# Token tiles moved by one DMA over 128 partitions instead of four over 32, and the lambda vectors loaded later

## The chip, the cores and the metric

One NeuronCore of a Trainium2 chip runs the whole program. The metric is device time in microseconds (us) of one execution; the time given for a kernel is the median of its runs. A profiled execution is one more run, recorded instruction by instruction, and has its own time.

## What is computed

Two layers of a hybrid backbone act on 1024 latent tokens `x` and 256 context tokens `ctx`, each token a row of 1024 float32 numbers. Layer 0 mixes tokens by differential attention, layer 1 by a bidirectional state-space layer (S5); each mixer is followed by a squared-ReLU MLP of width 4096, and both are wrapped in RMS norms with shift, scale and gate from a small projection of `c` ("ada").

```python
h = rmsnorm(x, norm_g[i, 0]) * (1.0 + s1) + sh1
y_lat, y_ctx = diff_attention(h_lat, h_ctx, ...) if i == 0 else s5_mixer(...)
x = x + g1 * rmsnorm(y_lat, norm_g[i, 1])
h = rmsnorm(x, norm_g[i, 2]) * (1.0 + s2) + sh2
x = x + g2 * rmsnorm(sqrelu_mlp(h, mlp_w1[i], mlp_w2[i]), norm_g[i, 3])
# in diff_attention:
lam = exp(sum(lf[0] * lf[1])) - exp(sum(lf[2] * lf[3])) + lambda_init
w = p[:, :, 0] - lam * p[:, :, 1]
```

The change touches how rows of `x`, `ctx` and two intermediate copies (`xa`, `xb`) travel between DRAM and SBUF, and when `lam` is computed.

## The kernel before

**Tokens and tiles.** The 1280 tokens form ten tiles of 128 (tiles 0 to 7 latent, 8 and 9 context). A token's number is taken apart as `8c + 2sh + sl`, with `sh` from 0 to 3 and `sl` 0 or 1. A tile holds one `sl` and 32 values of `c`; on the SBUF side its partition is `32 sh + c`. So in SBUF a tile is 128 partitions by 1024 numbers (4 KB a row, 512 KB in all), and in DRAM it is four blocks (`sh`), two tokens apart, of 32 rows, eight tokens apart. `tile_dma` (line 278) moves it as four DMAs of 32 partitions, 128 KB each. `pair_dma` (line 291) loads the two tiles with `sl` = 0 and 1 at once, as four DMAs of 256 KB: rows of 8 KB, 1 MB in all.

**Queue.** Every DMA is issued by `dma` (line 79) from one engine, SP, in one order. SP waits in that order for what each DMA needs, so a DMA that waits holds back all behind it. The order on SP and on the other engines is laid out when the program is built, by a planner with costs of its own, except inside `manual()` blocks, where the order of the source holds.

**Stages that the change and the prediction touch:**

- `setup` (line 155) and `lam_setup` (line 486) come first. `lam_setup` loads the four lambda vectors, broadcast to all partitions (128 KB into the buffer FC), and the sub-norm gains (0.5 KB), and computes `neglam`, `sg` and `ones` with nine small VectorE and two ScalarE instructions. Their first use is in the attention stage (lines 554, 672, 705).
- `phase_v` (line 339): V projection. `v_norm` (line 326) loads pairs 0 and 1 of `x` at the start, pairs 2 and 3 after the first group's products, pair 4 (context) after the second group's features; each tile is squared and summed on ScalarE (line 149), scaled on GpSimd (line 335), transposed on TensorE (line 314), modulated (lines 317, 319) and split into a high and a low part (lines 137, 138). The modulation needs `ada_w` (lines 237 to 263), and the products (lines 132 to 134) need split weights from `attn_w_qkv`. All these loads stand in SP's queue behind the first two pairs.
- `phase_b`: attention, in a hand-written order.
- `phase_c` (line 1246): output projection by `attn_w_o`, residual and MLP norm. `finish` (line 1260) loads tile `i` of `x` into one of three buffers, adds to it (line 1277), stores the sum to `xa` (line 1278), and takes its norm (line 1284). The load of the tile three places on goes into the same buffer, so it waits for that store. `feature` (line 1288) then transposes the finished tiles of a group; the last group's tiles go to `second_group` (line 1331).
- `mlp0_down` with `m0_tile` (line 1688): the first MLP's end. `first` loads a tile of `xa` (line 1700), `residual` adds it and stores tiles 0 to 7 to `xb` (line 1720). `mlp0_end` (line 1739) does the last five tiles in a hand-written order, with `xa` loads from line 1746, and hands over to the S5 stage, whose `rotate` (line 1853) writes over buffers that the last `xb` stores read.

Of the kernel before, what the change touches and what calls it, by code (L numbers as in the profile page):

```python
# [61 lines left out]
class Ring:  # L62
# [3 lines left out]
    def next(self):  # L66
        self.i += 1
        return self.items[self.i % len(self.items)]


class Prog:
# [206 lines left out]
    def tile_dma(self, dram, i, slot, store=False):  # L278

        d = dram[1] if i >= 8 else dram[0]  # L280
        src = d.rearrange("(c sh sl) d -> sl sh c d", sh=4, sl=2)[i % 2]
        if i < 8:
            src = src[:, 32 * (i // 2) : 32 * (i // 2) + 32]
        for sh in range(4):
            s = slot[32 * sh : 32 * sh + 32]
            if store:
                self.dma(src[sh], s)
            else:
                self.dma(s, src[sh])

    def pair_dma(self, dram, pair, slot):

        src = (dram[1] if pair == 4 else dram[0]).rearrange("(c sh sl) d -> sh c (sl d)", sh=4, sl=2)
        if pair < 4:
            src = src[:, 32 * pair : 32 * pair + 32]
        for sh in range(4):
            self.dma(slot[32 * sh : 32 * sh + 32].rearrange("p a b -> p (a b)"), src[sh])

    G_TOK = (512, 512, 256)
    G_TILES = ((0, 1, 2, 3), (4, 5, 6, 7), (8, 9))  # L300
# [38 lines left out]
    def phase_v(self):  # L339
        nc, I = self.nc, self.I  # L340
        self.xs = Ring([self.f0(8.5 + 8 * i, 2, 1024) for i in range(4)] + [self.fv(0, 2, 1024)])
        tmps = [Ring([v(o, 512), v(o + 2, 512)]) for v, o in ((self.fv, 0), (self.wv, 12), (self.wv, 12))]
        self.hT = self.hgroups()
        A, B = self.modc[:, 0, 1], self.modc[:, 0, 0]
        banks = [Ring([self.bank(i) for i in b]) for b in ((4, 6), (4, 6, 7), (4, 6, 7))]
        proj = Ring([self.bank(i) for i in range(4)])
        wr = [(self.rv(51 - 8 * i, 2, 512), self.rv(55 - 8 * i, 2, 512)) for i in range(4)]
        wt = [(hi[:, j], lo[:, j]) for hi, lo in wr for j in range(2)]
        wq = I["attn_w_qkv"][0].rearrange("(k p) n -> p k n", p=128)
        stg = Ring([self.rv(x, 2, 512) for x in (19, 23)])  # L350

        def load(ring, nb, order=range(4)):
            raws = [ring.next() for _ in order]
            for kk, raw in zip(order, raws):
                self.dma(shaped(raw, (2, 512)), wq[:, 2 * kk : 2 * kk + 2, 2048 + 512 * nb : 2560 + 512 * nb])
            return raws

        def weights(raws, order, engs):
            for raw, kk, eng in zip(raws, order, engs):
                hi, lo = wr[kk]  # L360
                self.split(hi, lo, shaped(raw, (2, 512)), eng)

        def feature(g, k, eng=None):
            m = 1 if g == 2 else 0
            self.to_feature(tiles[g], A[:, m], B[:, m], self.hT[g][0], self.hT[g][1], banks[g], tmps[g], k, eng, k % 2 == 1)

        def product(b, g, i, k, ks=range(8)):
            hh, hl = (t[:, k, 128 * i : 128 * i + 128] for t in self.hT[g])
            self.mm3(b, hh, hl, wt[k][0], wt[k][1], k == ks[0], k == ks[-1])

        def out(b, nb, g, i):
            kt = (2 + 4 * g + i) if g < 2 else i
            s = stg.next()
            nc.scalar.activation(s[:, 0], b, AF.Copy)
            nc.vector.tensor_tensor(s[:, 1], b, s[:, 0].bitcast(F32), ALU.subtract)
            for h in range(2):
                self.dma(self.Vd[4 * nb : 4 * nb + 4, h, :, kt].rearrange("h p e -> p h e"),
                         s[:, h].bitcast(F32).rearrange("p (h e) -> p h e", h=4))

        tiles = [self.v_norm(0)]  # L380
        acc = self.bank(5)
        for half in range(2):
            for seg in (1, 0):
                self.ada_half(0, seg, half, self.bank(5 if seg else 7))
            kk = range(2 * half, 2 * half + 2)
            weights(load(self.raw, 0, kk), kk, [nc.vector if half else nc.gpsimd] * 2)
        self.raw = Ring([self.wv(4 * i, 1024) for i in range(3)] + [self.view(self.SP, 4 * i, (1024,)) for i in range(3)])
        self.bg = [self.interleave([self.ada(0, seg, acc) for seg in (2, 3, 4)] + [self.rows_out(0, acc)],
                                   [self.s5_prep()])]
        bs = [proj.next() for _ in range(4)]  # L390
        for k in range(8):
            feature(0, k, nc.vector)
            for i in range(4):
                product(bs[i], 0, i, k)
        tiles.append(self.v_norm(1))
        for i in range(4):
            out(bs[i], 0, 0, i)
        for k in range(8):
            feature(1, k)
            self.step()  # L400
        tiles.append(self.v_norm(2))
        raws = load(Ring([self.f0(32.5, 1024), self.f0(36.5, 1024)]), 1, (3, 2))
        tok = [(g, i) for g in range(3) for i in range(len(self.G_TILES[g]))]
        for nb in range(2):
            for n, (g, i) in enumerate(tok[4 * (1 - nb) :]):
                if nb == 0 and n < 2:
                    for k in range(4 * n, 4 * n + 4):
                        feature(2, k)
                b = proj.next()
                ks = range(7, -1, -1) if (nb, n) in ((0, 5), (1, 0)) else range(8)  # L410
                for k in ks:
                    product(b, g, i, k, ks)
                if nb == 0 and n == 1:
                    raws += load(Ring([self.fv(0, 1024), self.fv(4, 1024)]), 1, (1, 0))
                elif nb == 0 and n == 5:
                    weights(raws, range(3, -1, -1), [None] * 4)
                out(b, nb, g, i)
                if nb and n == 1:
                    queries = self.b_start()
                if nb and n:  # L420
                    next(queries, None)
                self.step(6 if nb and n else 7)
        self.drain()
        for _ in queries:
            pass
# [59 lines left out]

    def lam_setup(self):
        nc, I = self.nc, self.I
        t, pr = self.fv(0, 256), self.fv(1, 2, 64)
        self.dma(t, I["attn_lambda"].rearrange("o a b -> o (a b)").to_broadcast((128, 256)))
        t4 = shaped(t, (2, 2, 64))  # L490
        nc.vector.tensor_tensor(pr, t4[:, :, 0], t4[:, :, 1], ALU.mult)
        st = self.lamc = self.cst.tile([128, 12], F32, name="lamc")
        nc.vector.tensor_reduce(st[:, 0:2], pr, AX.X, ALU.add)
        nc.scalar.activation(st[:, 2:4], st[:, 0:2], AF.Exp)
        nc.scalar.activation(st[:, 4:6], st[:, 2:4], AF.Ln)
        nc.vector.tensor_tensor(st[:, 4:6], st[:, 0:2], st[:, 4:6], ALU.subtract)
        nc.vector.tensor_scalar(st[:, 4:6], st[:, 4:6], 1.0, None, ALU.add)
        nc.vector.tensor_tensor(st[:, 2:4], st[:, 2:4], st[:, 4:6], ALU.mult)
        nc.vector.tensor_tensor(st[:, 6:7], st[:, 3:4], st[:, 2:3], ALU.subtract)
        nc.vector.tensor_scalar(st[:, 6:7], st[:, 6:7], -0.2, None, ALU.add)  # L500
        self.neglam = st[:, 6:7]
        self.dma(st[:, 7:8], I["attn_subln"].rearrange("o e -> e o"))
        nc.vector.tensor_scalar(st[:, 7:8], st[:, 7:8], 0.8, None, ALU.mult)
        self.sg = st[:, 7:8]
        self.ones = st[:, 8:9]
        nc.vector.memset(self.ones, 1.0)
# [937 lines left out]
    def a_out(self, run, p, t):  # L1444
        self.dma(self.A0[run][p], t)
# [908 lines left out]
    def run(self):  # L2354
        tc = self.tc
        pool = lambda name, **kw: tc.tile_pool(name=name, bufs=1, **kw)
        with pool("cst") as self.cst, pool("psp", space=bass.MemoryType.PSUM) as psp, \
# [22 lines left out]
            with pool("r0") as rp, pool("fc") as cp:  # L2380
                self.R, self.F = rp.tile([128, 59 * KB], F32R, name="R0"), cp.tile([128, 8 * KB], F32, name="FC")
                with pool("f0") as fp, pool("sp") as sp:
                    self.F0, self.SP = fp.tile([128, 41 * KB], F32, name="F0"), sp.tile([128, 12 * KB], F32, name="SP")
                    self.f0 = lambda off, *dims: self.view(self.F0, off, dims)
                    self.setup()
                    self.lam_setup()
                    more = [self.view(self.SP, 4 * i, (1024,)) for i in range(3)]
                    self.raw = Ring([self.wv(4 * i, 1024) for i in range(4)] + [self.f0(24.5 + 4 * i, 1024) for i in range(4)] + more)
                    self.phase_v()
# [78 lines left out]
```

## Time and profile before

| | |
|---|---|
| median of three runs | 2880.2 us (2878.24 to 2882.3) |
| the profiled execution's own time | 2870.1 us |
| its span, first to last instruction | 2868.3 us |
| mean granted TensorE clock | 0.989 |
| DMA queue of SP | 447564 packets, 583.53 MB, 63.9% of 16 engines' time |
| `x` in pairs | 16 DMAs of 256 KB from `x` and 4 from `ctx` |
| `x` and `ctx` in tiles | 40 DMAs of 128 KB |
| `xa` stores, `xa` loads, `xb` stores | 40, 40 and 32 DMAs of 128 KB |

Rows of the profile start with the time in us from the span's start and the duration, then engine, source line, operation, output and inputs; brackets give the idle time of the engine ahead of the instruction and what ended it. SP's DMA rows (SPq) are the issue alone. In a table by window, the columns are the busy us of each engine with its count, the granted clock (PEclk, 1.00 is full speed), the mean busy share of the 16 DMA engines, and GB/s.

### The profile page before, as it was taken

The numbers are of one execution on the slowest core, as the hardware profiler recorded it, in microseconds if no ns is written. First come the engines' busy times: TensorE is split into PE (matmuls) and PEld (weight loads), VectorE is DVE, ScalarE is ACT, GpSimd is POOL, SyncE is SP. The second block draws the span as 40 slices with busy tenths as digits, with TensorE's granted clock in tenths as the row PEclk, the third lists the DMA queues.
The fourth block names the chain that finished last, engine by engine and source line by source line (L and its number), as shares of the span: only waits on it lengthen the run. The fifth ranks groups of instructions, "written<-read, shape, count | busy, mean of one in ns | idle before, by whom it ended". The sixth has DMA issues, their size and how long they took to land. (4 is left out here: it accounts for less than half of the span.)

```text
span 2868.3 us, 43597 instructions
## 1 busy us (share of the span) xinstructions
PE 2730.3 (95%) x15225; PEld 2281.8 (80%) x15225; DVE 2016.2 (70%) x2968; ACT 1363.1 (48%) x2551; POOL 1021.6 (36%) x899
## 2 busy tenths in 40 slices
PE   7999999999899999999999999789999999999999
PEld 4688888888777887878877778688788778878887
DVE  5456788888863666666788767799533597668456
ACT  3425556555554743333444335477444633344443
POOL 2314666676663600000010013588121243336314
PEclk9999999999999999999999999899999999999999
DMA  9955555555826468885899887479743144466544
GB/s 299 309 169 175 153 173 175 177 175 169 255 83 190 120 212 306 296 305 192 272 294 299 260 244 242 156 232 295 253 140 110 59 159 164 158 235 235 165 131 141
DMA packets 447786, 586.33 MB, mean 204 GB/s; under 512 B 60494, under 2 KB 293196, under 8 KB 444364
## 3 DMA queue, kind: packets, MB, share of 16 engines
q1 hardware_dynamic: 447564, 583.53, 63.9%
q8 instruction: 120, 1.97, 0.3%
q14 instruction: 102, 0.84, 0.1%
HBM read 396.38 MB, written 182.82 MB: 202 GB/s over the span
## 5 line engine op out<-in xcount | busy, mean ns | idle before, releaser
L132 PE MATMUL PS<-H 128*128 128x512 f32 x1056 | 416.0, 395 | 8.6 <-DVE FD L1620 5.7
L134 PE MATMUL PS<-H 128*128 128x512 f32 x1056 | 413.8, 393 | 1.6 <-DVE H L2139 1.3
L133 PE MATMUL PS<-H 128*128 128x512 f32 x1056 | 414.8, 393 | 0.0
L132 PE MATMUL PS<-H,R 128*128 128x512 f32 (+1 forms) x828 | 307.5, 374 | 3.6 <-ACT R L137 1.6
L133 PE MATMUL PS<-H,R 128*128 128x512 f32 (+1 forms) x828 | 298.2, 360 | 1.4 <-POOL H L138 1.4
L134 PE MATMUL PS<-H,R 128*128 128x512 f32 (+1 forms) x828 | 297.6, 360 | 0.0
L132 PEld LDWEIGHTS PS<-H 128*128 128x128 f32 x1056 | 199.4, 189 | 55.0 <-issue 6.4
L134 PEld LDWEIGHTS PS<-H 128*128 128x128 f32 x1056 | 199.6, 189 | 45.3 <-DVE H L2139 1.7
L133 PEld LDWEIGHTS PS<-H 128*128 128x128 f32 x1056 | 199.7, 189 | 41.5 <-issue 1.0
L545 ACT ACTIVATE F<-F,stat 128x1280 f32<-128x1280 f32 x128 | 174.4, 1363 | 106.2 <-DVE F L535 105.9
L132 PE MATMUL PS<-R,H 128*128 128x512 f32 x536 | 213.6, 401 | 1.4 <-ACT R L137 1.4
L137 ACT ACTIVATE R<-W 128x512 fp32r<-128x512 f32 (+1 forms) x186 | 130.8, 712 | 172.3 <-PE PS L133 99.2
L133 PE MATMUL PS<-R,H 128*128 128x512 f32 x536 | 210.9, 394 | 0.0
L134 PE MATMUL PS<-R,H 128*128 128x512 f32 x536 | 209.3, 394 | 1.7 <-DVE H L138 1.7
L137 ACT ACTIVATE H<-U 128x640 fp32r<-128x640 f32 x216 | 132.9, 678 | 150.9 <-PE PS L133 104.5
L138 DVE TENSOR_TENSOR H<-W,H 128x512 fp32r<-128x512 f32 (+1 forms) x137 | 124.2, 917 | 103.8 <-ACT H L137 103.1
L138 DVE TENSOR_TENSOR H<-U,H 128x640 fp32r<-128x640 f32 x216 | 165.9, 805 | 39.7 <-ACT H L137 37.8
L535 DVE TENSOR_SCALAR_CACHE_REDUCE F<-PS 128x1280 f32<-128x1280 f32 x128 | 185.2, 1483 | 8.6 <-PE PS L522 8.4
L137 ACT ACTIVATE H<-W 128x512 fp32r<-128x512 f32 (+2 forms) x158 | 96.1, 616 | 191.2 <-PE PS L133 114.3
L132 PEld LDWEIGHTS PS<-H,R 128*128 128x128 f32 x828 | 156.8, 190 | 29.7 <-issue 4.1
L134 PEld LDWEIGHTS PS<-H,R 128*128 128x128 f32 x828 | 156.8, 189 | 25.4 <-issue 0.8
L582 POOL TENSOR_SCALAR R<-F 128x256 fp32r<-128x256 f32 (+1 forms) x128 | 127.1, 993 | 134.3 <-ACT F L581 121.5
(514 smaller groups left out, 6830.0 us busy)
## 6 DMA issues: line engine op xcount, KB each, us to landing
W<-in_mlp_w SPq DMA_DIRECT2D x176, 256.0 KB, 3.0
U<-Aa SPq DMA_DIRECT2D x108, 320.0 KB, 4.5
Aa<-FU SPq DMA_DIRECT2D x91, 320.0 KB, 4.6
Ad<-F SPq DMA_DIRECT2D x112, 256.0 KB, 3.0
W<-Ad SPq DMA_DIRECT2D x112, 256.0 KB, 2.8
FU<-in_mlp_w SPq DMA_DIRECT2D x32, 512.0 KB, 5.5
Ta<-FU SPq DMA_DIRECT2D x16, 1024.0 KB, 3.9
recd<-U SPq DMA_DIRECT2D x64, 256.0 KB, 4.8
```

Source lines behind the costliest of these rows:

```text
L132: mm(out, ah, bh, start=first, stop=False, **kw)
L133: mm(out, ah, bl, start=False, stop=False, **kw)
L134: mm(out, al, bh, start=False, stop=last, **kw)
L137: self.nc.scalar.activation(hi, src, AF.Copy)
L138: (lo_eng or self.nc.vector).tensor_tensor(lo, src, hi.bitcast(F32), ALU.subtract)
L535: ts(p[c], self.PS[:, 1280 * c : 1280 * c + 1280], 1.0, None, ALU.mult, ALU.min, accum_out=sm[:, c : c + 1])
L545: nc.scalar.activation(p[c], p[c], AF.Exp, bias=sm[:, c : c + 1], scale=-1.0, accum_out=sn[:, 0:1] if c else s0[:, u + 1 : u + 2])
L582: nc.gpsimd.tensor_scalar(hi, t, 1.0, 0.0, ALU.mult, ALU.add)
```

## The change

Both helpers hand the whole tile or pair to one DMA: the DRAM side is a pattern of 4 by 32 rows, the SBUF side all 128 partitions. This replaces 172 DMAs by 43. `lam_setup` moves from before `phase_v` to its loop over the second weight block: it stands after the split of those weights, and its scratch space is moved to a place in FC that this split has just read.

```diff
@@ tile_dma
-        for sh in range(4):
-            s = slot[32 * sh : 32 * sh + 32]
-            if store:
-                self.dma(src[sh], s)
-            else:
-                self.dma(s, src[sh])
+        if store:
+            self.dma(src, slot)
+        else:
+            self.dma(slot, src)
@@ pair_dma
-        for sh in range(4):
-            self.dma(slot[32 * sh : 32 * sh + 32].rearrange("p a b -> p (a b)"), src[sh])
+        self.dma(slot.rearrange("p a b -> p (a b)"), src)
@@ phase_v
                 elif nb == 0 and n == 5:
                     weights(raws, range(3, -1, -1), [None] * 4)
+                    self.lam_setup()
@@ lam_setup
-        t, pr = self.fv(0, 256), self.fv(1, 2, 64)
+        t, pr = self.fv(6, 256), self.fv(7, 2, 64)
@@ run
                     self.setup()
-                    self.lam_setup()
```

## Prediction, made before the changed kernel was run

> **What bounds the kernel now.** I read the page first (busy times, the 40 slices, the chain that ended last), then windows where these tiles move, then SP's order and who waits for what.
>
> ```profile
> span 2868.3 us, 43597 instructions
> PE 2730.3 (95%) x15225; PEld 2281.8 (80%) x15225; DVE 2016.2 (70%) x2968; ACT 1363.1 (48%) x2551; POOL 1021.6 (36%) x899
> PE   7999999999899999999999999789999999999999
> DMA  9955555555826468885899887479743144466544
> PE 29%; DVE 4%; DMA 2%; ACT 1%; issue 1%; POOL 0%; SPq 0%; DVEq 0%; POOLq 0%; ACTq 0%
> ```
>
> TensorE is busy 95% of the span, so a transfer costs time only where PE or the chain waits for it: slice 1 (PE 7, DMA 9) and slice 26 (PE 7, around 1830 us). SP's own issuing has no share of the chain (SPq 0%), so 129 issues fewer buy nothing by themselves.
>
> The price of a transfer comes from windows (columns: length, busy us of PE, PEld, DVE, ACT, POOL, clock, DMA share, GB/s).
>
> ```profile
> 4.00:16.00 12.00, 0.70 (x4) 0.47 (x3) 2.18 (x11) 3.67 (x7) 2.08 (x5) 1.00 0.96 196
> 20.00:45.00 25.00, 20.27 (x269) 13.44 (x272) 13.46 (x49) 7.57 (x10) 8.46 (x6) 1.00 1.05 405
> 50.00:62.00 12.00, 12.00 (x79) 8.98 (x78) 11.03 (x39) 6.27 (x11) 3.21 (x6) 1.00 1.00 231
> 908.25:911.80 3.55, 3.55 (x18) 2.93 (x17) 0.69 (x1) 3.50 (x7) 1.65 (x4) 1.00 0.55 148
> 908.00:966.00 58.00, 56.28 (x289) 47.33 (x287) 25.13 (x26) 40.81 (x86) 42.89 (x57) 1.00 0.56 157
> 1819.00:1845.00 26.00, 17.65 (x82) 15.49 (x80) 19.39 (x22) 13.36 (x21) 13.17 (x20) 0.80 0.93 294
> ```
>
> From 20 to 45 us the queue holds weight loads over 128 partitions: 405 GB/s with all 16 engines busy, 25.3 GB/s an engine. From 4 to 16 us it holds the first two pairs, in quarters of 32 partitions: as busy (0.96), but 196 GB/s. From 50 to 62 us (pairs 2 and 3) 231 GB/s. The present quarters hold all engines at about half rate. That is the gain there might be.
>
> **The unknown: over how many DMA engines one merged transfer spreads.** No row shows this shape. Its SBUF side starts with 128 partitions; its DRAM side starts with 4 blocks, whose rows (8 tokens apart inside a block, blocks 2 tokens apart) don't fold into 128 even steps. Every fast load of the windows has 128 outermost on both sides. The two bounds:
>
> - 16 engines: 405 GB/s, 2.6 us for a pair (1.05 MB), 1.3 us for a tile (0.524 MB).
> - 4 engines, one for each DRAM block: 101 GB/s, 10.4 us and 5.2 us, during which those four hold up their share of every later transfer.
>
> Now, a pair of the first two takes 5.35 us of all engines (2.10 of the window's 2.35 MB, so 10.7 of 12 us for both), and a tile 1.95 us (3.55 us at a share of 0.55, in which 148 GB/s is just one tile), with 1.6 us of fixed time about it. I take the **four-engine end**: if work is dealt out by outermost blocks, four is all that both sides have in common, and on the DRAM side, where the shapes differ, the nearest row is the present quarter (32 rows), not the 405 GB/s load. No row settles it, so the other end keeps a large chance.
>
> The Trainium skill, page "DMA: Bandwidth & Descriptors", section "Why a DMA increments its semaphore by 16 and not by 1", says that a DMA runs on the largest number of engines up to 16 that divides the outermost size of both sides; by it the merged DMA gets 4, and the sum is the one below (+55 us) and not the sum of the 16-engine end (-10 us). No run here shows that rule yet.
>
> **The change part by part, at four engines.**
>
> *First stage.*
>
> ```profile
> 2.85 0.58 SPq L80 DMA_DIRECT2D lamc<-in_attn_subln  x1
> 4.08 0.35 SPq L80 DMA_DIRECT2D FC<-in_attn_lambda  x1
> 4.47 3.29 SPq L80 DMA_DIRECT2D F<-in_x  x7
> 18.32 1.92 SPq L80 DMA_DIRECT2D SP<-in_attn_w_qkv  x2
> 29.97 1.06 ACT L137 ACTIVATE R<-SP 128x1024 fp32r<-128x1024 f32 x1 [10.26 <-DMA SP<-in_attn_w_qkv]
> 32.27 1.20 PE L132 MATMUL PS<-R,H 128*128 128x512 f32 x4
> 42.97 1.06 ACT L137 ACTIVATE R<-F 128x1024 fp32r<-128x1024 f32 x1 [4.45 <-DMA F<-in_attn_w_qkv]
> ```
>
> The first products (32.27) wait for weights that stand behind the pairs, and so does the second half (42.97). On four engines two pairs take 20.7 us where they take 10.7: **+10**. Less the lambda part: 0.93 us of issues ahead of or among the pairs, and 0.13 MB (0.3 us): **-1**.
>
> *Pairs 2 and 3.*
>
> ```profile
> 44.59 8.19 SPq L80 DMA_DIRECT2D F<-in_x  x8
> 61.79 1.06 ACT L149 ACTIVATE F<-F 128x1024 f32<-128x1024 f32 x1 [2.35 <-DMA F<-in_x]
> 65.61 0.49 PE L314 MATMUL PS<-ident,F 128*128 128x128 f32 x3
> 66.80 1.76 SPq L80 DMA_DIRECT2D FC<-in_ctx  x4
> L149 ACT ACTIVATE F<-FC x2: 1054/1058/1062, 95.0 to 96.2; 128x1024 f32<-128x1024 f32 x2
> ```
>
> ScalarE waits for pair 3 until 61.79, and its two tiles' norms (1.06 us of ScalarE each, then GpSimd) end as PE turns to their transposes at 65.61: no slack. Both pairs now take 9.1 us (2.10 of the 2.77 MB in 12 us); at 20.7 us they land 11.6 us later, of which I count **+9**, as the small DMAs among them run beside. Pair 4 is issued at 66.8 and first used at 95.0, 28 us for a transfer of 10.4: nothing.
>
> *Lambda, where it goes.*
>
> ```profile
> 8.52 0.29 DVE L491 TENSOR_TENSOR FC<-FC 128x128 f32<-128x128 f32 x1 [3.21 <-DMA FC<-in_attn_lambda]
> 128.20 1.21 DVE L138 TENSOR_TENSOR R<-FC,R 128x1024 fp32r<-128x1024 f32 x1
> 130.80 0.68 DVE L375 TENSOR_TENSOR R<-PS,R 128x512 fp32r<-128x512 f32 x1
> L554 DVE SCALAR_TENSOR_TENSOR stat<-FC,stat,lamc x80: 219/220/533, 226.1 to 851.3; 128x1 f32<-128x1 f32 x80
> ```
>
> Its DMAs join SP's queue after the split that reads FC (128.20). It issues two DMAs, nine VectorE instructions (none over the 0.29 us of L491) and two of ScalarE. The first VectorE one waits for the DMA; behind it in VectorE's order stand evacuations like L375 (130.80), and PE waits for these only when all four product banks are full. First use is at 226.1. Cost nothing, as PE has other banks; without that cover the 4.4 us from issue (4.08) to L491 (8.52).
>
> *Output projection.*
>
> ```profile
> 890.11 1.06 ACT L137 ACTIVATE RT<-W 128x1024 fp32r<-128x1024 f32 x1 [9.78 <-DMA W<-in_attn_w_o]
> 908.25 1.73 SPq L80 DMA_DIRECT2D xa<-W  x4
> 911.81 1.71 SPq L80 DMA_DIRECT2D W<-in_x  x4
> 963.28 1.28 DVE L1277 SCALAR_TENSOR_TENSOR W<-FA,stat,W 128x1024 f32<-128x1024 f32 x1 [1.48 <-POOL stat L144]
> 969.37 0.49 PE L314 MATMUL PS<-ident,FA 128*128 128x128 f32 x3
> ```
>
> Two tile loads stand among the `attn_w_o` loads for which ScalarE waits (890.11): 2 x (5.2 - 1.95) = 6.5 us on four engines, partly beside other work: **+4**. Then ten stores and seven loads follow from 908 on. Now they take 17 x 1.95 = 33 us of 58 (share 0.56) and nothing waits. On four engines they take 17 x 5.2 = 88 us: the last load, with three stores after it, ends at about 908 + 0.7 + 14 x 5.2 = 981 at best, and the last residual needs it at 963.28: +18. Each load also waits in SP's queue for the store out of its buffer (911.81 behind 908.25), with the next stores and the MLP weights queued behind it: up to 7 x 1.6 us more, +29. PE transposes that tile (969.37) and works in order. I take **+22**. Below: nothing, if the last load beats 963; but that needs 14 transfers in 55 us, 3.9 us each.
>
> *MLP end.*
>
> ```profile
> 1819.22 3.97 SPq L80 DMA_DIRECT2D FD<-xa  x8
> 1837.73 1.95 SPq L80 DMA_DIRECT2D xb<-FD  x4
> L80 SPq DMA_DIRECT2D H<-xa x8: 317/420/1337, 1421.2 to 1752.4; - x8
> 1844.51 0.82 DVE L1853 TENSOR_TENSOR FD<-PS,FD 128x640 f32<-128x640 f32 x1 [2.13 <-DMA xb<-FD]
> ```
>
> From 1819 to 1845 five tiles move (two `xa` loads, three `xb` stores; 2.62 of 7.64 MB). On four engines they need 26 us, and the rest's share 5.02 MB / 405 GB/s = 12.4 us: 38 us where there are 26. VectorE waits at 1844.51 for the last of these stores already, so what is later counts in full: +12, less what is queued behind that store: **+9**. The thirteen earlier transfers of this stage (eight loads, the first at 1421, and five stores) add 13 x 3.25 = 42 us to four engines over 400 us, with loads far ahead of their use: **+2**.
>
> Sum: 10 - 1 + 9 + 4 + 22 + 9 + 2 = **+55 us**. Against the profiled execution (2870.1 us, of which 1.8 us lie around the span) that is 2925; it ran 10 us below the median of the runs, 2880.2, to which I add the same 55: **2935 us**. By the bounds of the steps (0 to +10 where four engines may be faster than counted, +29 in the output projection, +12 at the MLP's end) this case reaches from 2905 to 2968.
>
> **The rivals.**
>
> *Sixteen engines: faster.* One DMA then fills all partitions at 405 GB/s. First stage 10.7 to 5.2 us and the lambda part: -6.5. Pairs 2 and 3: nothing, since PE is busy 12.00 of 12 us there. `attn_w_o` -1.3; the MLP's end the whole wait of 2.13, no more, since other work ends there. Sum -10: **2870**. For it: the SBUF side has the shape of the 405 GB/s loads, and the same bytes now hold the engines twice as long. Against: the DRAM side. It decides if a merged pair lands in under 5 us. The Trainium skill, same page, section "Rules for kernel authors", advises one 128-partition transfer in place of two on halves; by that advice alone this case is the one. The windows agree that 32-partition transfers are slow (196 against 405 GB/s).
>
> *Four engines, but later stages are covered.* The first stage cannot hide it (+9); if the plan puts the loads of the output projection earlier or other products in between, little of the rest shows, say the MLP's end: +18, **2898**. Against: three buffers, and a share near 1.0 on the four engines for 88 us.
>
> *The merged DMA works through its four blocks one after another on all engines*, as the quarters do: durations stay, the lambda part and 1.5 us of issues at the MLP's end go: -2.5, **2878**.
>
> **How the numbers follow.** Four engines as summed 0.53, covered 0.14, sixteen 0.26, block after block 0.07. This kernel's measurement tells about 0.2% (5.8 us) from no change. Faster: 0.8 of the sixteen-engine case and 0.2 of the last: 0.22. Same: most of the rest of these two and a little of the covered case: 0.10. Slower: 0.68. The range must reach the sixteen-engine case, since 0.26 is more than may be left out: 2866 (a little under 2870) to 2968, leaving out some 0.12; the likeliest case alone is 2905 to 2968.
>
> **What would show it.** In the first window: under four engines the DMA share from 5 us on falls to some 0.3 while only pairs move, and the first products start at about 41 us; under sixteen they start near 26 us. A lone `xa` store at 908 us takes 5 us of packets at a share of 0.25 (four) or 1.3 us near 1.0 (sixteen). In the output projection L1277 would wait for the DMA from `x`, which it never does now. VectorE's wait at L1853 grows by some 9 us or goes. I am wrong if one tile takes under 3 us of packets, or if PE stays busy from 908 to 966 us although the share is a quarter.

## The result and the profile after

Over five runs each, the changed kernel takes 3033.2 us (median; 3029.8 to 3036.7) and the kernel before 2878.5: a ratio of 1.054, 95% interval 1.052 to 1.056. It is **155 us slower**, beyond the range of the prediction. The profiled execution of the changed kernel took 3036.7 us, with a span of 3034.9 against 2868.3, so 166.6 us are to be found in the two traces. Lines of the source after 300 stand 2 or 3 lower than before (L314 is now L311, L1277 is L1275, L1853 is L1851).

The page of the changed kernel, the same rows as before, and the granted clock in its 40 slices:

```profile
span 3034.9 us, 43390 instructions
PE 2765.6 (91%) x15225; PEld 2304.9 (76%) x15225; DVE 2008.3 (66%) x2968; ACT 1361.7 (45%) x2551; POOL 1013.0 (33%) x899
PE   4799999999898589999999998858999999999999
PEclk9899999999999799999999999979999999999999
DMA  7666465555824238896699985458945135458544
```

A slice is 76 us. PE has three valleys: the first two slices (4 and 7 in place of 7 and 9), the 13th to 15th (910 to 1140 us: 8, 5, 8, where it was at 9), and the 25th to 28th (1820 to 2125 us: 8, 8, 5, 8 in place of a single 7 and 8). They are the three places where tiles and pairs move, and the clock falls in each, to 8, 7 and 7; before, one slice alone showed less than 9 (an 8). DMA in the first two slices is 7 and 6 in place of 9 and 9: the engines are *less* busy where the kernel waits for them.

The windows that answer to those of before, and the middle of the second one (length, busy us of PE, PEld, DVE, ACT, POOL, clock, DMA share, GB/s):

```profile
4.00:16.00 12.00, 0.52 (x2) 0.18 (x1) 0.65 (x3) 1.07 (x1) 0.00 (x0) 1.00 0.57 121
961.90:972.10 10.20, 10.20 (x48) 8.41 (x46) 2.68 (x4) 6.99 (x14) 5.17 (x9) 1.00 0.19 53
964.50:967.50 3.00, 3.00 (x15) 2.49 (x14) 1.39 (x2) 0.97 (x1) 2.12 (x3) 1.00 0.28 59
961.00:1068.00 107.00, 68.91 (x307) 56.22 (x305) 23.03 (x27) 39.66 (x84) 37.47 (x58) 0.82 0.23 81
1961.00:1992.00 31.00, 12.71 (x58) 10.62 (x56) 18.97 (x21) 12.61 (x20) 11.55 (x16) 0.72 0.58 166
```

The first window is not the pairs alone, since `ada_w` loads are issued from 4.14 us on; its share does not count a pair's engines. The second is a lone `xa` store, from its issue to the next issue, which waits for it: 10.2 us where it was 3.55. In its middle (964.5 to 967.5, the third row) the share is 0.28 at 59 GB/s: close to four engines of sixteen (0.25). The share times length times 16 is the time that the engines spent on the tile: 10.2 x 0.19 x 16 = 31 engine-us. The quarters of before spent 3.55 x 0.55 x 16 = 31 engine-us as well. The work is the same; it stands on a quarter of the engines.

The first stage, in SP's issues, ScalarE's waits and PE's first product (start, duration, in brackets the idle time ahead and what ended it):

```profile
2.88 1.22 SPq L80 DMA_DIRECT2D F<-in_x  x2
4.14 21.40 SPq L80 DMA_DIRECT2D W<-in_ada_w  x4
25.59 13.92 SPq L80 DMA_DIRECT2D F<-in_ada_w  x4
40.05 1.95 SPq L80 DMA_DIRECT2D SP<-in_attn_w_qkv  x2
...
65.28 4.02 SPq L80 DMA_DIRECT2D F<-in_x  x2
```

```profile
24.20 1.06 ACT L149 ACTIVATE F<-F 128x1024 f32<-128x1024 f32 x1 [19.13 <-DMA F<-in_x]
38.99 1.06 ACT L149 ACTIVATE F<-F 128x1024 f32<-128x1024 f32 x1 [12.46 <-DMA F<-in_x]
50.22 1.06 ACT L137 ACTIVATE R<-SP 128x1024 fp32r<-128x1024 f32 x1 [8.90 <-DMA SP<-in_attn_w_qkv]
...
95.57 1.06 ACT L149 ACTIVATE F<-F 128x1024 f32<-128x1024 f32 x1 [7.39 <-DMA F<-in_x]
```

```profile
52.82 1.18 PE L132 MATMUL PS<-R,H 128*128 128x512 f32 x4
```

The first pair, issued at 2.88, is there at 24.20, 21.3 us later; the second 14.8 us after it. The `ada_w` rows of the kernel before are:

```profile
8.41 4.14 SPq L80 DMA_DIRECT2D W<-in_ada_w  x4
13.45 4.29 SPq L80 DMA_DIRECT2D F<-in_ada_w  x4
```

SP now takes 21.40 us from the first to the last of four issues that took 4.14, and 13.92 over four that took 4.29, and comes to `attn_w_qkv` at 40.05 (before: 18.32). PE's first product starts at 52.8 in place of 32.3, and pair 3 ends ScalarE's wait at 95.57 in place of 61.79.

The output projection in SP's order, and the waits of its window and of the handover to S5 (engine, line, what it waited for: us in total, times, longest):

```profile
961.94 0.56 SPq L80 DMA_DIRECT2D xa<-W  x1
972.15 0.55 SPq L80 DMA_DIRECT2D W<-in_x  x1
972.75 0.54 SPq L80 DMA_DIRECT2D xa<-W  x1
985.96 0.54 SPq L80 DMA_DIRECT2D W<-in_x  x1
```

```profile
DVE W L1275 <- DMA W<-in_x: 48.8, 5, 13.0
DVE FA L1275 <- DMA FA<-in_x: 17.7, 2, 9.9
```

```profile
DVE FD L1851 <- DMA xb<-FD: 16.4, 1, 16.4
```

Each load (972.15, 985.96) is issued when the store out of its buffer has landed; a store and a load then share the four engines for 13.8 us, and so it goes tile by tile. The window of one such store and load:

```profile
972.10:986.00 13.90, 13.90 (x65) 11.43 (x64) 4.86 (x6) 8.37 (x18) 6.77 (x13) 1.00 0.21 75
```

The two tiles cost 13.90 x 0.21 x 16 = 47 engine-us together, 23 a tile: less than the lone store's 31. VectorE waits 67 us for tiles of `x` for which it never waited, and 16.4 us at L1851 where it waited 2.13.

The rows of the tiles `xa` and `xb` (count, ns of one issue, first and last start in us) give milestones, first for the kernel before, then for the changed one:

```profile
L80 SPq DMA_DIRECT2D xa<-W x28: 302/421/648, 908.2 to 965.9; - x28
```

```profile
L80 SPq DMA_DIRECT2D xb<-FD x16: 302/418/458, 1724.3 to 1839.3; - x16
```

```profile
L80 SPq DMA_DIRECT2D xa<-W x7: 512/528/557, 961.9 to 1067.6; - x7
```

```profile
L80 SPq DMA_DIRECT2D xb<-FD x4: 537/562/2106, 1838.8 to 1991.5; - x4
```

By the first and last `xa` store and the last `xb` store the span splits into four parts. The table also holds the experiments below, as differences from the kernel before, each from one profiled execution. The two rows in even rows have the same transfers and still differ by 4.5 us up to the first `xa` store, so differences of a few us are not resolved:

| kernel | to first `xa` store | to last `xa` store | to last `xb` store | to the end | span |
|---|---|---|---|---|---|
| before (us) | 908.2 | 57.7 | 873.4 | 1029.0 | 2868.3 |
| changed | +53.7 | +48 | +50.5 | +14.4 | +166.6 |
| pairs only | +42.4 | 0 | -3 | +3 | +42.4 |
| tiles only | +6 | +51 | +59 | +14 | +130 |
| `xa` in even rows | +44 | +22 | +2 | +14 | +82 |
| eight blocks | +25 | +12.5 | +14 | +9 | +61 |
| all in even rows (`even_rows`) | -6 | -1.6 | -8 | +3 | -12.7 |
| the same transfers (`even_rope`) | -1.6 | -1.6 | -8.6 | +2 | -9.7 |
| mixed | -2.4 | -1.5 | -6 | +5 | -4.9 |

### The profile page after: what moved, and what is told of

The parts are those of the page before. It is cut to its first block, busy times and chain, and to the rows that moved or that the text cites. A ratio compares the mean times of both kernels' runs of the same rounds, so it can differ in the third digit from the quotient of the medians.

```text
span 3034.9 us, 43390 instructions
## 1 busy us (share of the span) xinstructions
PE 2765.6 (91%) x15225; PEld 2304.9 (76%) x15225; DVE 2008.3 (66%) x2968; ACT 1361.7 (45%) x2551; POOL 1013.0 (33%) x899
## 5 line engine op out<-in xcount | busy, mean ns | idle before, releaser
L133 PEld LDWEIGHTS PS<-H 128*128 128x128 f32 x1056 | 201.2, 191 | 42.4 <-issue 1.0
L132 PEld LDWEIGHTS PS<-H,R 128*128 128x128 f32 x828 | 156.8, 190 | 30.8 <-issue 4.1
L134 PEld LDWEIGHTS PS<-H,R 128*128 128x128 f32 x828 | 156.7, 189 | 25.3 <-issue 0.8
L133 PEld LDWEIGHTS PS<-H,R 128*128 128x128 f32 x828 | 157.3, 190 | 21.8 <-POOL H L138 1.7
```

What stands on the lines that cost most here:

```text
L132: mm(out, ah, bh, start=first, stop=False, **kw)
L133: mm(out, ah, bl, start=False, stop=False, **kw)
L134: mm(out, al, bh, start=False, stop=last, **kw)
```

## The experiments

**Theory S**: a DMA is dealt out over as many DMA engines as both sides have outermost blocks in common, so the merged ones get four, and these four are the loss. The Trainium skill, page "DMA: Bandwidth & Descriptors", section "Why a DMA increments its semaphore by 16 and not by 1", states it as the largest number up to 16 that divides both outermost sizes. **Rivals**: P, the planner lays the program out anew and that costs the time; L, lambda's new place; M, one large DMA is slow whatever its DRAM side; later E, W and H, told in their runs.

**lam_only and merge_only: which half of the change.** `lam_only` is the kernel before with the three lambda hunks of the change alone; `merge_only` is the changed kernel without them.

> Four quarters are kept, only the lambda part is moved. Theory S (the loss is the merged transfers' spread over four DMA engines): 2877 us, -1 against before, within 0.2%. Rival P (the plan that is laid out anew with another list of instructions costs the time): the order of TensorE's work changes here too, so 20 us or more of the +155 show. Rival L (lambda's wait on VectorE holds back evacuations): +5 to +15, with idle VectorE ahead of the lambda product near 135 us.

> All transfers merged, lambda left at the start. Theory S: 3033 us within 10, all of the +155. Rival L: 10 us or more below the changed kernel.

Measured: `lam_only` 0.9988 of the kernel before, interval 0.9973 to 1.0004 (2871.4 us), no difference; in its trace the lambda product waits 0.28 us for its DMA at 134.5 us and holds up nobody. `merge_only` 3035.7 us, ratio 1.0565 (1.0542 to 1.0588). All of the loss is the merging; L falls, and P for this half.

**even_rows: the same DMAs with another DRAM side.** Other tokens stand in a tile, so this kernel does not compute the reference; the number and size of its transfers stay. In the changed kernel:

```diff
-        src = d.rearrange("(c sh sl) d -> sl sh c d", sh=4, sl=2)[i % 2]
+        src = d.rearrange("(c sl) d -> sl c d", sl=2)[i % 2]
         if i < 8:
-            src = src[:, 32 * (i // 2) : 32 * (i // 2) + 32]
+            src = src[128 * (i // 2) : 128 * (i // 2) + 128]
```

and the same in `pair_dma`.

> The changed kernel, with the same single DMA for each tile and pair, but over 128 rows with one even step in DRAM, so that both sides have 128 outermost; the tokens of a tile are other ones, so the order of the tokens in the computation is not that of the reference. Theory S: the merged transfers run on all 16 engines, a lone xa store is near a share of 1.0 for 1.3 to 2 us, the first products start near 26 us, 2870 us (2860 to 2885). Rival M (one large DMA in place of four is slow whatever its DRAM side): 3033 us within 30, share of a lone store 0.25. Rival P (the new plan costs the time): its plan is nearly that of the changed kernel, so 2920 us or more with the share near 1.0.

Measured: 2855.9 us, ratio 0.9937 (0.9915 to 0.9960), 4 us below the range expected. The windows of the first stage, of a lone `xa` store, and of its middle:

```profile
4.00:16.00 12.00, 4.38 (x54) 2.58 (x53) 0.65 (x3) 5.64 (x9) 5.94 (x11) 1.00 1.00 378
902.00:905.60 3.60, 3.60 (x17) 3.00 (x16) 0.75 (x2) 3.48 (x7) 1.62 (x4) 1.00 0.36 146
903.00:904.00 1.00, 1.00 (x6) 0.84 (x5) 0.00 (x0) 0.97 (x5) 0.59 (x2) 1.00 1.01 418
```

Share 1.01 and 418 GB/s while the store runs: sixteen engines. PE's first product starts at 26.2 us, where the prediction had it for sixteen engines. The plan is nearly that of the changed kernel, so P falls too, and so does M. The advice of the Trainium skill (same page, "Rules for kernel authors") to use one 128-partition transfer agrees with this run, and not with the changed kernel: it needs the 128 rows on the DRAM side too.

**halves and blocks8: the number of blocks as a dose.** Two DMAs of 64 partitions (two blocks each), and one DMA with eight blocks of 16 rows, which again puts other tokens into a tile. Each edit is shown for `tile_dma`; `pair_dma` has the same:

```diff
-        if store:
-            self.dma(src, slot)
-        else:
-            self.dma(slot, src)
+        for sh in (0, 2):
+            s = slot[32 * sh : 32 * sh + 64]
+            if store:
+                self.dma(src[sh : sh + 2], s)
+            else:
+                self.dma(s, src[sh : sh + 2])
```

```diff
-        src = d.rearrange("(c sh sl) d -> sl sh c d", sh=4, sl=2)[i % 2]
-        if i < 8:
-            src = src[:, 32 * (i // 2) : 32 * (i // 2) + 32]
+        src = d.rearrange("(q c e sl) d -> q sl e c d", c=16, e=8, sl=2)[i // 2 if i < 8 else 0, i % 2]
```

> The changed kernel, but two DMAs of 64 partitions (two blocks of 32 rows in DRAM) for each tile and pair. Theory S, the engines being as many as the outermost blocks: two engines for each half; if both halves get the same two, a lone tile takes twice the 8.9 us at a share near 0.12 and the time is 3150 us or more; if they get different ones, it stays at 3033 within 30. Rival M (size of a DMA decides): between before and after, 2900 to 2980 us.

> The changed kernel, but the one DMA of a tile or pair has 8 blocks of 16 rows in DRAM (2 tokens apart, rows 16 apart) in place of 4 of 32; the tokens of a tile stand in another order, so what is computed is not the reference. Theory S, engines as many as outermost blocks, each tile costing 31 engine-us as in the kernel before: a lone xa store at a share of 0.5 for some 4 to 5 us, a pair 10.7 us; that is the price that the prediction had used for four engines (5.2 and 10.4 us), so its steps are tried at their own price: 2930 us if their sum (+55) holds, 2890 to 2940 in all. Rival (any pattern that doesn't fold into one step gets four engines): share 0.25 and 3033 us within 30. Rival (sixteen for eight blocks): share near 1.0 and 2860 to 2880 us.

Measured: `halves` 3223.8 us, ratio 1.121 (1.119 to 1.123); `blocks8` 2932.9 us, ratio 1.020 (1.017 to 1.023). First SP's issues of the first two pairs in `halves` and a window in which only they move, then a lone `xa` store of `blocks8` and its middle:

```profile
2.85 13.21 SPq L80 DMA_DIRECT2D F<-in_x  x4
4.00:16.00 12.00, 0.46 (x2) 0.18 (x1) 0.65 (x3) 1.18 (x1) 0.00 (x0) 1.00 0.13 32
```

```profile
933.50:939.50 6.00, 6.00 (x29) 4.95 (x28) 1.91 (x2) 3.71 (x8) 2.89 (x5) 1.00 0.35 90
935.00:937.00 2.00, 2.00 (x10) 1.65 (x9) 0.69 (x1) 1.95 (x5) 1.43 (x3) 1.00 0.49 88
```

Shares of 0.13 (two of sixteen), and 0.49 (eight), beside 0.28 and 1.01 above: as many engines as blocks. Both halves stand on the same two engines, since the share stays at 0.13 while SP issues four of them in the window. The Trainium skill's rule (page "DMA: Bandwidth & Descriptors", the section named under Theory S) agrees with all four. At eight blocks the tile costs 6.00 x 0.35 x 16 = 34 engine-us, that is 4.2 us on eight engines, somewhat below the 5.2 that the prediction had for four. PE's first product starts at 43.4 us, where the prediction had 41 for its price.

**even_rope and even_quarters: is it the even rows or the merging?** `even_rope` is `even_rows` with the rope tables' columns in the new order (the line below); `even_quarters` is `even_rope` with four DMAs of 32 partitions again.

```diff
-    order = tok.reshape(4, 32, 4, 2).transpose(0, 3, 2, 1).reshape(-1)
+    order = tok.reshape(4, 32, 4, 2).transpose(0, 3, 1, 2).reshape(-1)
```

> The run even_rows with the columns of the rope tables (constants) put in the tiles' new order of tokens, so that the reference is computed again; no other edit. Theory S: as even_rows, 2856 us within 6, ratio 0.994, faster than the kernel before and the changed one. Rival W (even_rows was fast because of its other data): 2870 us or more.

> even_rope, but each tile and pair again by four DMAs of 32 partitions (32 even rows in DRAM each). It tells whether even_rows gained by the merging or by the even rows. Theory S, 32-partition transfers holding the engines longer whatever the DRAM side (31 engine-us a tile in the kernel before, 22 in even_rows): 2872 us within 6, the first products near 32 us, share from 4 to 16 us near 0.96 at some 196 GB/s. Rival E (even rows in DRAM are the gain): 2856 us within 6, 330 GB/s or more there.

Measured: `even_rope` 2856.5 us, ratio 0.9936 (0.9916 to 0.9956). The expectation is mistaken in one thing: the S5 stage transposes 32 partitions at a time and so still takes the tokens in another order than the reference's; the work is the same. So it cannot by itself rule out W, that other data made it fast; but `even_quarters` has the same data and takes 13 us more, and `mixed_even` below, which keeps the reference's order, is faster than the kernel before too. `even_quarters` 2869.2 us, ratio 0.9978 (0.9964 to 0.9991). Its first stage and a lone `xa` store:

```profile
4.00:16.00 12.00, 1.16 (x8) 0.50 (x8) 0.65 (x3) 4.30 (x7) 3.74 (x6) 1.00 1.01 243
906.20:909.80 3.60, 3.60 (x18) 2.98 (x17) 0.69 (x1) 3.48 (x7) 1.71 (x4) 1.00 0.54 146
```

The store costs 3.60 x 0.54 x 16 = 31 engine-us, as before; merged over 128 even rows it was 3.60 x 0.36 x 16 = 21. So most of the gain (0.0042 of 0.0064) is the merging, and E falls as the main cause; even rows help the first stage somewhat (243 GB/s against 196).

**pairs_only and tiles_only: the parts.** Only `pair_dma`, or only `tile_dma`, as in the change.

> Only the pairs are merged (five DMAs over 4 by 32 rows); tiles in quarters, lambda at the start. Theory S with the price taken from the tile's own engine time: the first xa store comes some 54 us later, as in the changed kernel, and nothing is given back: 2929 us within 12. Rival (the plan or later stages absorb half): 2900 us or less.

> Only the tiles are merged; pairs in quarters, lambda at the start. Theory S: first xa store as before (908 us within 8), then +50 in the output projection and +51 at the end of the first MLP: 2976 us within 12. With pairs_only it adds up to the +155 of the changed kernel. Rival (late transfers cost because the early ones have shifted the plan): 2950 us or less.

Measured: `pairs_only` 2913.9 us, ratio 1.0141 (1.0115 to 1.0167), so about +40 us; `tiles_only` 2994.1 us, 1.0418 (1.0392 to 1.0445), about +120. Both expectations were missed, by 15 and 18 us in opposite directions. Of the 54 us up to the first `xa` store, which I had all put down to the pairs, some 6 to 11 belong to the two tile loads among the `attn_w_o` loads (+6 in `tiles_only`, 53.7 - 42.4 = 11; each from one execution). Together the two give 0.0559, the changed kernel 0.0541: the parts add up.

**act_pairs: is SP's holding a cost of its own?** In the changed kernel:

```diff
-        self.dma(slot.rearrange("p a b -> p (a b)"), src)
+        (self.nc.scalar if pair < 2 else self.nc.sync).dma_start(out=slot.rearrange("p a b -> p (a b)"), in_=src)
```

> The changed kernel with the first two pairs issued from ScalarE's queue; it tells whether the 20 us by which the first products come later are the four engines' time or SP being held at issue behind the pairs. Theory S, the four engines' own time: every weight load needs these four too, the first products stay near 52.8 us, 3033 us within 8. Rival H (SP held is a cost of its own): the weights are issued by 10 to 20 us, the first products start near 42 us or earlier, 3008 to 3022 us.

Measured: 3038.5 us, ratio 1.0561 (1.0529 to 1.0593), no gain. SP's issues of `ada_w` in the first 45 us (ns of one: least, median, most), of the changed kernel and then of `act_pairs`; then SP's waits and ScalarE's there:

```profile
L80 SPq DMA_DIRECT2D W<-in_ada_w x4: 479/5397/9997, 4.1 to 17.6; - x4
```

```profile
L80 SPq DMA_DIRECT2D W<-in_ada_w x4: 368/552/894, 3.0 to 22.5; - x4
```

```profile
SPq L80 <- DMA F<-in_x: 33.4, 2, 17.5
```

```profile
47.87 1.06 ACT L137 ACTIVATE R<-SP 128x1024 fp32r<-128x1024 f32 x1 [5.22 <-DMA SP<-in_attn_w_qkv]
```

The run does **not** decide it cleanly. In the changed kernel single issues take up to 10.0 us: SP is held at issue. In `act_pairs` they take at most 0.9, but SP now waits twice, 33.4 us in all, for the pairs' DMA, so that the weights come as late as before (47.87 in place of 50.22). The first product starts at 50.8, 2 us earlier, without effect on the end. What bounds the cost of the holding is the changed kernel's own trace: the second pair's norms start at 38.99 us, and PE turns to the last two of the group's transposes at 45:

```profile
44.99 0.69 PE L311 MATMUL PS<-ident,F 128*128 128x128 f32 x2 [0.41 <-POOL F L332]
```

Without any holding the products could hardly start before these, so it is worth at most some 8 of the 20.5 us. That is argued, not shown, and it bounds the first products alone. Behind pairs 2 and 3 SP is held once more, at the one issue ahead of pair 4 (before, then changed):

```profile
58.13 6.81 SPq L80 DMA_DIRECT2D F<-in_s_c_re  x1
75.39 22.49 SPq L80 DMA_DIRECT2D F<-in_s_c_re  x1
```

What that holding is worth was not tried; H stays open as to its size. It is no rival to Theory S as the root: over even rows, on sixteen engines, the same number of DMAs loses nothing (`even_rows`).

**after_xa_tiles: one kind of transfer given back.** In the changed kernel, `xa` lies in DRAM tile by tile:

```diff
-            self.xa = dt("xa0", 1024, 1024), dt("xa1", 256, 1024)
+            self.xa = dt("xa0", 10, 128, 1024)
@@ tile_dma
+        if dram is self.xa:
+            self.dma(dram[i], slot) if store else self.dma(slot, dram[i])
+            return
```

> The changed kernel, but xa, which only these tiles use, lies in DRAM tile by tile, 128 rows in one step; pairs, loads of x and stores to xb keep the 4 blocks. Theory S: xa moves on 16 engines, 1.4 us of packets; what is left on four engines is one load a tile in the output projection (cadence 10 us or less in place of 13.8) and one store a tile at the MLP's end. First xa store as in the changed kernel (about 955 to 962), the output projection costs 15 to 30 in place of 51 and the MLP 10 to 25 in place of 51: 2960 us, 2940 to 2985. Rival (the loads of x alone hold up the stage): 3000 us or more.

Measured: 2952.1 us, ratio 1.0262 (1.0232 to 1.0292), half of the loss gone. The total is as expected; the MLP's loss of 2 us up to its last `xb` store is less than the 10 to 25 expected for the MLP, with 14 more at its end. The `xa` store alone:

```profile
952.50:956.00 3.50, 3.50 (x17) 2.92 (x16) 0.69 (x1) 3.46 (x7) 1.60 (x4) 1.00 0.37 150
```

3.50 us, 21 engine-us. By the table the output projection keeps +22, what loads of `x` on four engines cost, and the MLP up to its last `xb` store falls from +50.5 to +2: there the `xa` transfers were the cost, and the eight `xb` stores, still on four engines, cost only the wait at the end (+14).

**mixed_even: a version that beats both.** The kernel before, with pairs over 128 even rows, `xa` as above and `xb` likewise. The order of the tokens is put back where PSUM is read in the first stage. Parts of the edit, with the rest left out at the dots:

```diff
+            o = t.rearrange("p (i sh c) -> p i sh c", sh=4, c=32)
+            y = y.rearrange("p (i c sh) -> p i sh c", sh=4, c=32)
...
@@ glu_done
-            self.dma(x, self.xb[0].rearrange("(c t) d -> t c d", t=8)[t])
+            for q in range(4):
+                self.dma(x[32 * q : 32 * q + 32], self.xb[2 * q + t % 2, 32 * (t // 2) : 32 * (t // 2) + 32])
```

> A version that computes the reference with 128 even rows on both sides wherever the layout allows: from the kernel before, pairs over 128 even rows in one DMA (the order of the tokens put back by strided reads of PSUM in the evacuation of the first stage's transposes), xa and xb in DRAM tile by tile with one DMA a tile, loads of x in the output projection still in quarters, and the later loads of xb now in quarters. Theory S: the first stage gains the 6 us that it gained in even_rows, and most of the gain at the MLP's end, 2860 us within 6, ratio 0.995, faster than both kernels. Rival (the strided reads or the quartered loads of xb give it back): 2870 us or more.

Measured: 2863.6 us, ratio 0.9960 (0.9944 to 0.9977): faster than both kernels, and than the kernel before by 0.4%, less than `even_rows`. The first product starts at 28.2 us. In its trace the first `xa` store comes 2.4 us earlier than before, and 5 us are lost after the last `xb` store, where the quartered loads of `xb` stand. Neither is resolved as an effect: `even_rope` too shows 1.6 us where `even_rows` shows 6, and `pairs_only` and `even_rows` lose 3 us at the end without such loads.

## Why the prediction was wrong

**Right:** the direction, the four engines, and the places: the first stage, the loads of `x` at L1275, VectorE's wait at L1851. Lambda at nothing was right (`lam_only`). The three rivals fell: sixteen engines by the shares, the covered case by the three valleys, block after block by the share of 0.28.

**The step that failed is the price**, "On four engines they take 17 x 5.2 = 88 us" and the 10.4 us of a pair. I took the rate of an engine from the 405 GB/s weight loads (25.3 GB/s), but the tiles' own rows, quoted in the same prediction, gave another: 1.95 us of all engines is 31 engine-us, 7.8 us on four; 5.35 us a pair is 21.4 us on four. The lone store measured 31 engine-us. Of the first two pairs the first took 21.3 us and the second 14.8 more, 18 each on average. So the true price lay well above mine, though it is not one number: a store and a load that run together cost 23 engine-us a tile, 5.9 us on four. I had written down that the quarters hold the engines at half rate, and then let merged blocks run at the full one. Alone, only the transfers with 128 even rows in DRAM do that (21 engine-us). My signs of being wrong did not look for this: they asked for a tile of under 3 us, and none for one slower than 5.2.

The price explains much of the size. In `blocks8` a lone tile takes 4.2 us where I had 5.2, and the whole comes close to my sum: 2932.9 us (+59 beside its own runs of the kernel before) against my 2935 (+55). That agreement is partly luck. The parts are +25, +12.5 and +14, then +9 behind, against my +22 (10 - 1 + 9 + 4), +22, +11 and nothing, and the second pair is there 27.2 us after the first one's issue (2.85 to 30.05), where I had 20.7 for the two.

The upper end of my range was not worked out either: the bounds that I named add 7 us (29 for 22) and 3 us (12 for 9) to the 2935, which makes 2945 and not 2968.

Step by step:

- *First stage*, predicted +10 and +9: `pairs_only` shows +42. In the changed kernel the first product comes 20.5 us later, pair 3 is normed 34 us later, and pair 4, which I had at nothing, 41.5 us later (136.57 in place of 95.03), as SP issues it 33 us later (100.23 in place of 66.80). ScalarE does not wait for its DMA.
- *`attn_w_o` loads*, +4: 6 to 11 by the two partial runs.
- *Output projection*, +22, at most +29: +48. The chain of a load that waits for the store of its buffer, which I counted at most at 7 x 1.6 us, runs at 13.8 us for each store and load. The form of this step held: on a straight line from `blocks8` (a lone tile 4.2 us, +12.5) to the changed kernel (7.8 us, +48), my 5.2 us stands at +22 (an estimate from these two runs). Its price failed.
- *The thirteen earlier transfers at the MLP's end*, +2 since "loads far ahead of their use": this failed in its reasoning too. Up to the last `xb` store the MLP loses 50.5 us, and `after_xa_tiles` takes 48 of it away. The same straight line, from +14 to +50.5, gives +24 at 5.2 us, where I had +11 for the whole MLP; so here the price was not all. The transfers are not spread over 400 us but come in clusters. One of them holds four `xb` stores and four `xa` loads; its first and last issues, before and after:

```profile
1724.29 3.60 SPq L80 DMA_DIRECT2D xb<-FD  x8
...
1759.24 2.36 SPq L80 DMA_DIRECT2D FD<-xa  x4
```

```profile
1838.83 0.58 SPq L80 DMA_DIRECT2D xb<-FD  x1
...
1893.89 0.55 SPq L80 DMA_DIRECT2D FD<-xa  x1
```

  35 us before, 55 after: eight tiles at 5.9 to 7.8 us hold the four engines for 47 to 62 us, and loads go into buffers whose stores must have ended.
- *MLP end*, +9: VectorE's wait grew by 14.3 us, a little over the +12 bound.

## What to carry to other kernels

Before merging DMAs, look at the outermost dimension of *both* sides: one DMA over 128 partitions whose DRAM side begins with 4 blocks ran on 4 engines here, and cost its full engine time there. Price a transfer that moves to fewer engines by its own engine time (length x share x 16 of its own row) and not by the best rate in the trace, and keep a margin: that was right for a lone tile (31 engine-us) and too high for a store and a load together (23 a tile). The gain of merging is there (31 to 21 engine-us a tile), but it needs a DRAM layout with 128 even rows, which a private buffer such as `xa` can be given.

## What the runs showed that I had not expected

PE was not only idle longer; its busy time grew too. The same 15225 matmuls kept PE busy for 2765.6 us in place of 2730.3: 35 of the 166.6 us are busy time, beside a mean granted clock of 0.967 in place of 0.989, and of 0.82 and 0.72 in the windows 961 to 1068 and 1961 to 1992 us. The records do not separate that from other causes of longer matmuls.

SP can be held at issue where its waits show no semaphore: up to 10.0 us for one `ada_w` issue behind two merged pairs (the median was 0.37 in the kernel before), and 22.49 us for the issue of `in_s_c_re` (6.81 before). And an engine's rate depends on the pattern: 31 to 34 engine-us for a lone tile in quarters or in merged blocks, 23 a tile for a store and a load together on four engines, 21 for 128 even rows, with the same 4 KB rows in all of them. Why was not settled.
